# Attention biases in a two-layer hybrid decoder: made one head group at a time, spread in DRAM four heads at a time

## The chip, the cores and the metric

The kernel runs on one core of a Trainium2 chip. The time is device microseconds of one execution of the whole program; the kernel before has a median of 2954.24 us over three runs (2948.36 to 2954.89). The engines are TensorE (PE; its weight loads are listed as PEld), VectorE (DVE), ScalarE (ACT), GpSimd (POOL) and SyncE (SP). SP and POOL issue the DMAs.

## The reference

One sequence of 1024 tokens with 1024 channels passes two layers. Layer 0 mixes tokens by a gated delta rule, layer 1 by dilated sliding-window attention; each is followed by a SwiGLU, and each sub-layer has an RMS norm with shift, scale and gate from a condition. The change touches layer 1 alone:

```python
DSW_GROUPS = ((128, 1), (512, 4), (2048, 16))      # (window, dilation); 8 heads of 64 channels in each
proj = (h @ w_in).reshape(Bsz, S, 3, 3, 8, 64)     # queries, keys, values; group; head
q = rms_norm(proj[:, :, 0], q_gain) * 64 ** -0.5
k = rms_norm(proj[:, :, 1], k_gain)
v = proj[:, :, 2]
# in each group: query t attends to keys t, t-d, ..., t-window
logits = q @ k + bias_table[t5_causal_bucket(dist * dilation)]   # one bias for each head and distance
p = softmax(where(valid, logits, -inf)); o = p @ v
# the three groups' outputs are merged by their softmax denominators, then @ w_out
```

For each group and head the bias depends on the distance between query and key only. For a tile of 128 queries and 256 keys it is a band matrix: row p is a vector of 383 numbers shifted by p.

## The kernel before, in words

All products are float32 made of three products of a high and a low part (`split3`: `wh*hh + wh*hl + wl*hh`). The program is written in an order; a planner then orders each engine's instructions by its own account of when each is ready, earlier written ones first, and each engine runs its instructions strictly in that order. SP's queue of DMA issues is such an order too: an issue that waits holds up all issues behind it.

Layer 1 works in six units (`units`, line 1731): group 0, 2, 1, and in each the lower and the upper four heads (`hq`). A unit computes its queries, keys and values (`attn_proj`, line 1538, called at 1733 to 1735), each 1024 tokens by 256 channels in four pieces `t2` of 256 tokens, and then goes over eight tiles of 128 queries (`attn_unit`, line 1571): logits into a PSUM bank `pt`, logits plus bias with a row maximum on VectorE (line 1606), exponentials on ScalarE, transposes into bank `pp`, products with the values into bank `ob`. For the first unit, pieces 0 and 1 of all three kinds are computed in the stage ahead (`pre`), and lie in PSUM until they are copied out. Queries and keys are squared, summed and scaled (lines 1551 to 1556), transposed in bank `tq`, and copied to SBUF (lines 1566, 1568).

Weights are loaded by SP in pieces of 256 KB into raw tiles `wraw` (line 185); ScalarE makes the high part (line 187), VectorE and POOL in turn subtract it to make the low part (`lo_of`, line 161). Two kinds of buffers take turns, two weight units each (`wpools`): one with four raw tiles and one, `wps`, with a single raw tile, so that there a load starts only when the piece before it has been split. The first unit's values and the second unit's keys use `wps`.

PSUM has eight banks, in this stage `banks(pd="a", pt="b", pp="c", tq="d", ob="e")`, with two banks behind a, b and c and one behind d and e. Bank b holds the keys made ahead when the stage begins.

The biases come from `bias_rows` (line 1491), called behind the first unit's values (line 1737). For each group, one product of the table with a one-hot matrix (`oh`, loaded at line 1486) in a bank `pt` gives 8 vectors of 383; VectorE copies them to a tile `bv`, whose buffers it shares with the squares of the queries and keys (`sqv`, three buffers), and POOL stores them in DRAM (`v_d`). Then, for each group, one POOL transfer within DRAM copies each vector 128 times (`b_d`, 1532 KB). `attn_unit` loads a tile of four heads' biases from there, with each row shifted by one number (line 1577, on SP), into one of two buffers.

Of the kernel before, what the change touches and what calls it, by code (L numbers as in the profile page):

```python
# [10 lines left out]
F32 = mybir.dt.float32  # L11
# [6 lines left out]
P = 128  # L18
# [14 lines left out]
VL = 383  # L33
# [35 lines left out]
def trunk(tc, A, out, stop=None):  # L69
    nc = tc.nc  # L70
    V, G, ACT, SP = nc.vector, nc.gpsimd, nc.scalar, nc.sync
# [28 lines left out]
    def pool(name, bufs=1, **k):  # L100
        return tc.tile_pool(name=name, bufs=bufs, reuse_waits="tile", **k)
# [5 lines left out]
    def scratch(name, shape):  # L107
        if stop is not None:
            return nc.dram_tensor(name, shape, F32, kind="ExternalOutput").ap()
        return dr.tile(list(shape), F32, name=name)  # L110

    ps = es.enter_context(pool("ps", 1, space=PSUM))
    bank = {}
# [12 lines left out]
    def pt():  # L126
        return bank["pt"]()
# [10 lines left out]
    def rsqrt(o, i, n, half=0):  # L138
        G.tensor_tensor(o, i, pw[:, half, :n], ALU.pow)
# [393 lines left out]
    with ExitStack() as ga:  # L533
# [482 lines left out]
        src = [[], []]  # L1016
# [363 lines left out]
    def attn_products(g, hq, kind, t2s, hT, pd_, wk=None):  # L1380

        wk = wk or attn_weights(g, hq, kind)
        for t2 in t2s:
            o = pd_()
            for j in range(2):
                hf, tk = toks(g, 2 * t2 + j)
                split3(o[:, j * 256:(j + 1) * 256],
                       [((hT[hf][k][0][:, tk], hT[hf][k][1][:, tk]),
                         (wk[k // 4][0][:, k % 4], wk[k // 4][1][:, k % 4])) for k in range(KT)])
            yield (kind, t2), o  # L1390
# [65 lines left out]
    def quad(kind):  # L1456
        return qp.tile([P, 2048], F32, name="qkv", tag="qkv%d" % kind)
# [13 lines left out]
    with ExitStack() as da:  # L1471
# [3 lines left out]
        ap_ = da.enter_context(pool("da", 2))  # L1475
        ROW = DH + 2

        bias_d = [scratch("v_d", (3, 8, VL)), scratch("b_d", (3, 8, P, VL))]
        og_d = scratch("og_d", (S, 2, 2, 4 * ROW))
        ou0 = ap_.tile([P, NCH, 2, 4, ROW], F32, name="ou0", bufs=1)  # L1480

        def t2k(name, *shape, tag=None, bufs=2):
            return ap_.tile([P, *shape], F32, name=name, tag=tag or name, bufs=bufs)

        oh = ap_.tile([BUCKETS + 1, 3, VL], F32, name="oh", tag="gl")
        SP.dma_start(oh.rearrange("p g n -> p (g n)"), A["k_oh"])
        rel = ap_.tile([BUCKETS + 1, 24], F32, name="rel", bufs=1)
        V.memset(rel[BUCKETS:BUCKETS + 1], 1.0)
        SP.dma_start(rel[0:BUCKETS], A["rel_bias"])

        def bias_rows():

            for g in range(3):
                b = pt()
                PE.matmul(b[0:8, 0:VL], rel[:, g * 8:(g + 1) * 8], oh[:, g], start=True, stop=True)
                bv = ap_.tile([8, VL], F32, name="bv", tag="sqv", bufs=3)
                V.tensor_copy(bv, b[0:8, 0:VL])
                G.dma_start(bias_d[0][g], bv)
            for g in range(3):
                G.dma_start(bias_d[1][g], bias_d[0][g][:, None, :].to_broadcast([8, P, VL]))  # L1500

        def reorder(views):

            spare = [t_[:, j] for t_ in (ap_.tile([P, 2, HALF], F32R, name="hs", tag="gl") for _ in range(2))
                     for j in range(2)] if not spares else spares
            for k in range(KT):
                new = [[], []]
                for i in range(2):
                    old = [hT[h][k][i] for h in range(2)]
                    for at in range(2):  # L1510
                        new[at].append(spare.pop(0))
                        for h in range(2):
                            o, x = views(new[at][i], at, old[h].bitcast(F32), h)
                            if i == 0:
                                ACT.activation(o, x, AF.Copy)  # L1515
                            else:
                                V.tensor_copy(o, x)
                    spare += old
                for h in range(2):
                    hT[h][k] = tuple(new[h])  # L1520
            spares[:] = spare
# [16 lines left out]
        def attn_proj(g, hq, kind):  # L1538
            if (g, hq) == (0, 0):
                todo = chain((((kind, t2), pre[kind, t2]) for t2 in range(2)),  # L1540
                             attn_products(g, hq, kind, range(2, 4), hT, pd, pre["w"] if kind == 0 else None))
            else:
                todo = attn_products(g, hq, kind, range(4), hT, pd)
            res = quad(kind)
            for (_, t2), o in todo:
                if kind == 2:
                    ACT.activation(res[:, t2 * HALF:(t2 + 1) * HALF], o, AF.Copy)
                    continue
                sqv = t2k("sqv", 8, DH, bufs=3)
                ov = o.rearrange("p (a b) -> p a b", b=DH)  # L1550
                ACT.activation(sqv, ov, AF.Square)
                ss = ap_.tile([P, 2, 8], F32, name="ssa", tag="ssa", bufs=3)
                V.tensor_reduce(ss[:, 0], sqv, axis=mybir.AxisListType.X, op=ALU.add)
                V.tensor_scalar(ss[:, 0], ss[:, 0], 1.0 / DH, EPS, op0=ALU.mult, op1=ALU.add)
                rsqrt(ss[:, 1], ss[:, 0], 8)
                V.tensor_tensor(sqv, ov, ss[:, 1, :, None].to_broadcast([P, 8, DH]), ALU.mult)
                qf = sqv.rearrange("p a b -> p (a b)")
                b = bank["tq"]()
                for hp in range(2):
                    for j in range(2):  # L1560
                        PE.transpose(b[:, (hp * 2 + j) * P:(hp * 2 + j + 1) * P],
                                     qf[:, j * 256 + hp * P:j * 256 + (hp + 1) * P], ident)
                d = res.rearrange("p (h t c) -> p h t c", h=2, t=NCH)[:, :, 2 * t2:2 * t2 + 2]
                bv = b.rearrange("p (h t c) -> p h t c", h=2, t=2)
                if kind == 0:
                    ACT.activation(d, bv, AF.Copy)
                else:
                    ACT.activation(d, bv, AF.Copy, scale=gqk)
            return res

        def attn_unit(g, hq, q, k, v, half_done):
            bias = ap_.tile([P, 4, 256], F32, name="bias", tag="bias")
            src = bias_d[1][g, hq * 4]

            def load(p0, n, c0):

# [13 lines left out]
            for at, t in enumerate(order):  # L1590
# [23 lines left out]
                ob = bank["ob"]()  # L1614
                for i in range(2):
                    b = bank["pp"]()
                    bv = b.rearrange("p (h w c) -> p h w c", h=2, w=2)
# [9 lines left out]
                    for hp in range(2):  # L1627
                        h = 2 * hp + i
                        for w in range(w0, 2):
                            PE.matmul(ob[:, h * DH:(h + 1) * DH], pT[:, hp, w], vv[:, t - 1 + w, h * DH:(h + 1) * DH],  # L1630
                                      start=w == w0, stop=w == 1)
# [13 lines left out]
        src = [[], []]  # L1645
# [84 lines left out]

        units = [(g, hq) for g in (0, 2, 1) for hq in range(2)]
        for g, hq in units:
            q = attn_proj(g, hq, 0)
            k = attn_proj(g, hq, 1)
            v = attn_proj(g, hq, 2)
            if (g, hq) == units[0]:
                bias_rows()
            if (g, hq) in ((0, 1), (2, 1)):
                reorder(mod16 if g == 0 else mod4)
            attn_unit(g, hq, q, k, v, half_done if (g, hq) == units[-1] else None)  # L1740
# [57 lines left out]
def program(inputs, stop=None):  # L1798
    import concourse.bacc as bacc
    nc = bacc.Bacc("TRN2", target_bir_lowering=False, num_devices=1, dynamic_dma_scratch_size=8192)  # L1800
    arrays = {n: np.ascontiguousarray(inputs[n]) for n in _INS}
    arrays["k_sq"], arrays["k_oh"] = shape_constants()
    aps = {n: nc.dram_tensor(f"in_{n}", a.shape, mybir.dt.from_np(a.dtype), kind="ExternalInput").ap()
           for n, a in arrays.items()}
    out = nc.dram_tensor("out_0", (1, S, D), F32, kind="ExternalOutput").ap()
    with tile.TileContext(nc, schedule_with_timeline_sim=True) as tc:
        trunk(tc, aps, out, stop)
    return nc, {f"in_{n}": a for n, a in arrays.items()}
# [7 lines left out]
```

## Time and profile before

| | |
|---|---|
| median of three runs | 2954.24 us |
| the profiled execution | 2960.85 us |
| its span, first to last instruction | 2959.0 us |
| mean granted TensorE clock | 0.961 |
| PE busy | 2774.2 us, 94% |
| PEld busy | 2355.6 us, 80% |
| DVE busy | 1686.9 us, 57% |
| ACT busy | 1078.8 us, 36% |
| POOL busy | 584.4 us, 20% |
| weight loads of layer 1's attention | 68 of 256.0 KB, 2.9 us from issue to landing |

Times inside the span count from its start. A share of busy time is an average over stages with different limits; a stage is read from its own window. [...] A DMA issue is short; its transfer is told by the time to landing.

### The profile page before, as it was taken

Reading aid. Unit: us, or ns where it says so; the run is one execution under the profiler, and the core shown is the slowest. Engines: PE = TensorE matmul, PEld = TensorE weight load, DVE = VectorE, ACT = ScalarE, POOL = GpSimd, SP = SyncE. Lnnn points to the kernel's source line nnn. Section 1 sums busy time; section 2 is a strip of 40 time slices with the busy share of each in tenths; the row PEclk is TensorE's granted clock in tenths of the full one; section 3 lists DMA queues with packets and bytes.
Section 4 is the critical chain, followed back from the end, with each engine's and each line's share of the span. In section 5 each row is a group of like instructions: output and inputs, shape, how many; then the busy total and the mean of one; then the engine's idle time right before and its main releaser. Section 6 shows DMA issues by size and latency. Waiting matters only on the chain.

```text
span 2959.0 us, 40301 instructions
## 1 busy us (share of the span) xinstructions
PE 2774.2 (94%) x15207; PEld 2355.6 (80%) x15207; DVE 1686.9 (57%) x3387; ACT 1078.8 (36%) x2187; POOL 584.4 (20%) x644
## 2 busy tenths in 40 slices
PE   6989888888999999999999899999978999999999
PEld 5767776776877888878889789999966788888887
DVE  7875676664586666677454333332368655557443
ACT  5432333332363333332133453353335433334110
POOL 2151415141202111100014112322211111111000
PEclk8989999899999999999999989999979999999999
DMA  7333432234734344375222311111223222237211
GB/s 260 95 92 111 113 88 72 57 90 142 236 113 142 122 136 126 121 262 184 73 75 75 92 29 32 51 48 46 85 91 105 75 82 85 80 114 235 86 43 57
DMA packets 299679, 312.16 MB, mean 105 GB/s; under 512 B 35683, under 2 KB 219747, under 8 KB 299484
## 3 DMA queue, kind: packets, MB, share of 16 engines
q1 hardware_dynamic: 288140, 278.16, 30.7%
q0 software_dynamic: 11344, 31.43, 3.3%
q8 instruction: 119, 1.95, 0.3%
q14 instruction: 76, 0.62, 0.1%
HBM read 250.55 MB, written 63.66 MB: 106 GB/s over the span
## 4 chain that ended last, share of the span: by engine, by line
PE 68%; DMA 10%; DVE 9%; POOL 3%; ACT 3%; issue 3%; SPq 0%; DVEq 0%; POOLq 0%; ACTq 0%
PE pd L79 33%; PE u L79 14%; PE v L79 7%; PE pt L79 4%; PE y L79 4%; DMA araw<-in_w_ada 3%; PE ob L79 2%; POOL U L802 1%; POOL Ut L800 1%; PE p L79 1%; DVE w L161 1%; DVE acc L227 1%; DMA E<-gs_d 1%; PE sc L79 1%; PE pp L79 1%
## 5 line engine op out<-in xcount | busy, mean ns | idle before, releaser
L79 PE MATMUL pd<-hl,w 128*128 128x512 f32 x4248 | 1072.3, 405 | 22.0 <-ACT w L187 7.9
L79 PEld LDWEIGHTS pd<-hl,w 128*128 128x128 f32 x4248 | 799.5, 194 | 189.9 <-ACT w L187 8.8
L79 PE MATMUL pd<-w,hl 128*128 128x256 f32 x2880 | 390.6, 288 | 4.5 <-ACT hl L1515 3.8
L79 PEld LDWEIGHTS pd<-w,hl 128*128 128x128 f32 x2880 | 363.3, 194 | 11.7 <-ACT hl L1515 4.9
L79 PE MATMUL u<-hx,wo 128*128 128x512 f32 x1056 | 254.6, 391 | 5.1 <-ACT ft L1252 3.7
L161 DVE TENSOR_TENSOR w<-wraw,w 128x512 fp32r<-128x512 f32 (+1 forms) x243 | 197.0, 822 | 93.4 <-ACT w L187 65.6
L79 PEld LDWEIGHTS u<-hx,wo 128*128 128x128 f32 x1056 | 198.5, 188 | 47.5 <-ACT ft L1252 4.1
L187 ACT ACTIVATE w<-wraw 128x512 fp32r<-128x512 f32 (+1 forms) x171 | 107.8, 645 | 214.4 <-DMA wraw<-in_gdn_w_in 100.8
L227 DVE SCALAR_TENSOR_TENSOR acc<-araw,vecT,acc 128x512 f32<-128x512 f32 x140 | 110.0, 786 | 92.1 <-DMA araw<-in_w_ada 91.5
L1362 DVE SCALAR_TENSOR_TENSOR qkv<-pd,modT,qkv 128x512 f32<-128x512 f32 x96 | 71.5, 749 | 123.0 <-PE pd L79 123.0
L161 DVE TENSOR_TENSOR wo<-ss,wo 128x512 fp32r<-128x512 f32 x88 | 83.6, 957 | 92.4 <-ACT wo L1199 90.7
L79 PE MATMUL u<-hl,w 128*128 128x512 f32 x528 | 130.3, 396 | 0.7 <-DVE qkv L487 0.7
L79 PE MATMUL v<-hl,wo 128*128 128x512 f32 x528 | 126.9, 390 | 0.4 <-DVE ft L1254 0.4
L79 PE MATMUL y<-hl,w 128*128 128x512 f32 x528 | 127.2, 390 | 0.0
L79 PE MATMUL v<-hx,wo 128*128 128x512 f32 x528 | 126.6, 389 | 0.0
L79 PE MATMUL u<-hl,wo 128*128 128x512 f32 x480 | 117.5, 394 | 5.0 <-ACT ft L1252 5.0
L1606 DVE CUSTOM_DVE_ANT_0 p<-pt,bias 128x128 f32<-128x128 f32 (+1 forms) x192 | 57.4, 348 | 112.8 <-PE pt L79 65.9
L688 DVE SCALAR_TENSOR_TENSOR yv<-raw,vecT,yv 128x512 f32<-128x512 f32 x144 | 114.2, 793 | 12.8 <-ACT yv L686 12.0
L79 PEld LDWEIGHTS u<-hl,w 128*128 128x128 f32 x528 | 100.9, 192 | 22.3 <-issue 1.1
L1222 POOL TENSOR_TENSOR ss<-wraw 128x512 f32<-128x512 f32 x30 | 42.5, 1416 | 385.1 <-PE u L79 310.0
L161 POOL TENSOR_TENSOR w<-wraw,w 128x512 fp32r<-128x512 f32 (+1 forms) x35 | 50.4, 1441 | 345.0 <-ACT w L187 345.0
L79 PEld LDWEIGHTS v<-hl,wo 128*128 128x128 f32 x528 | 99.0, 188 | 21.4 <-DVE ft L1254 0.8
(377 smaller groups left out, 4267.6 us busy)
## 6 DMA issues: line engine op xcount, KB each, us to landing
araw<-in_w_ada SPq DMA_DIRECT2D x160, 256.0 KB, 2.8
wraw<-in_w_ffn_in SPq DMA_DIRECT2D x66, 512.0 KB, 3.9
wraw<-in_dsw_w_in SPq DMA_DIRECT2D x68, 256.0 KB, 2.9
wraw<-in_w_ffn_out SPq DMA_DIRECT2D x34, 512.0 KB, 4.8
wraw<-in_gdn_w_in SPq DMA_DIRECT2D x66, 256.0 KB, 2.9
ft<-a_d SPq DMA_DIRECT2D x44, 256.0 KB, 3.8
qkv<-in_w_ffn_in SPq DMA_DIRECT2D x22, 512.0 KB, 3.9
qkv<-a_d SPq DMA_DIRECT2D x44, 256.0 KB, 3.4
```

Of the source, the lines that this page charges most:

```text
L79: i = f(*a, **k)
L161: e.tensor_tensor(o, x, hi.bitcast(F32), ALU.subtract)
L187: ACT.activation(hi, raw, AF.Copy)
L227: V.scalar_tensor_tensor(acc, raw, condT[:, k:k + 1], acc, op0=ALU.mult, op1=ALU.add)
L688: V.scalar_tensor_tensor(yv, raw[:, i:i + HALF], convT[:, i, ct:ct + 1], yv, op0=ALU.mult, op1=ALU.add)
L800: G.tensor_tensor(t, U[:, 0:m, m:m + 1].to_broadcast([64, m, n]), U[:, m:m + 1, m + 1:32].to_broadcast([64, m, n]), ALU.mult)
L802: G.tensor_tensor(U[:, 0:m, m + 1:32], U[:, 0:m, m + 1:32], t, ALU.add)
L1222: (V if i < 2 else G).tensor_tensor(s["s1"], a21, a22, ALU.add)
L1362: V.scalar_tensor_tensor(xt, o, modT[:, l, 5, n:n + 1], xt, op0=ALU.mult, op1=ALU.add)
L1606: V.tensor_tensor_reduce(p_[i][:, hp, c0:], lg[i][:, hp * 256 + c0:hp * 256 + 256], bias[:, h, c0:], 1.0, -3.0e38, ALU.add, ALU.max, orow[ ...
```

## The change

`bias_rows` makes one group at a time. It is called three times within the first unit: group 0 behind the queries, group 2 behind the keys, group 1 behind the values. Its product goes to a bank `ob`. Each group has DRAM tensors of its own, and the upper and lower four heads each have their own spread tensor and their own transfer (766 KB). Store and spreads are issued by SP in place of POOL. `attn_unit` loads from the spread of its own four heads.

```diff
-        bias_d = [scratch("v_d", (3, 8, VL)), scratch("b_d", (3, 8, P, VL))]
+        bias_d = [scratch("v%d_d" % g, (8, VL)) for g in range(3)]
+        spread_d = [[scratch("b%d%d_d" % (g, q), (4, P, VL)) for q in range(2)] for g in range(3)]
@@
-        def bias_rows():
-
-            for g in range(3):
-                b = pt()
-                PE.matmul(b[0:8, 0:VL], rel[:, g * 8:(g + 1) * 8], oh[:, g], start=True, stop=True)
-                bv = ap_.tile([8, VL], F32, name="bv", tag="sqv", bufs=3)
-                V.tensor_copy(bv, b[0:8, 0:VL])
-                G.dma_start(bias_d[0][g], bv)
-            for g in range(3):
-                G.dma_start(bias_d[1][g], bias_d[0][g][:, None, :].to_broadcast([8, P, VL]))
+        def bias_rows(g):
+
+            b = bank["ob"]()
+            PE.matmul(b[0:8, 0:VL], rel[:, g * 8:(g + 1) * 8], oh[:, g], start=True, stop=True)
+            bv = ap_.tile([8, VL], F32, name="bv", tag="sqv", bufs=3)
+            V.tensor_copy(bv, b[0:8, 0:VL])
+            SP.dma_start(bias_d[g], bv)
+            for q in range(2):
+                SP.dma_start(spread_d[g][q], bias_d[g][q * 4:q * 4 + 4, None, :].to_broadcast([4, P, VL]))
@@
-            src = bias_d[1][g, hq * 4]
+            src = spread_d[g][hq][0]
@@
-            q = attn_proj(g, hq, 0)
-            k = attn_proj(g, hq, 1)
-            v = attn_proj(g, hq, 2)
-            if (g, hq) == units[0]:
-                bias_rows()
+            qkv = []
+            for kind in range(3):
+                qkv.append(attn_proj(g, hq, kind))
+                if (g, hq) == units[0]:
+                    bias_rows((0, 2, 1)[kind])
+            q, k, v = qkv
```

## Rows read from the trace of the kernel before

**Rows 1.** The page: busy time of TensorE; the chain that ended last, by engine.
```profile
PE 2774.2 (94%) x15207; PEld 2355.6 (80%) x15207; DVE 1686.9 (57%) x3387; ACT 1078.8 (36%) x2187; POOL 584.4 (20%) x644
...
PE 68%; DMA 10%; DVE 9%; POOL 3%; ACT 3%; issue 3%; SPq 0%; DVEq 0%; POOLq 0%; ACTq 0%
```
**Rows 2.** Waits, 1560 to 1720: engine, line, releaser: total us, times, longest.
```profile
DVE p L1606 <- DMA bias<-b_d: 16.9, 1, 16.9
...
POOL b_d L1500 <- DMA v_d<-bv: 13.8, 1, 13.8
...
PE pt L79 <- DVE ou L1606: 9.8, 1, 9.8
```
**Rows 3.** Waits of SP's queue of issues, the same stretch.
```profile
SPq L1577 <- DMA b_d<-v_d: 23.3, 1, 23.3
```
**Rows 4.** Chain of waits, 1560 to 1720: start us, us, what.
```profile
1613.29 2.65 DMA v_d<-bv
1615.94 1.79 issue
1617.73 18.39 DMA b_d<-v_d
1636.18 4.76 DMA bias<-b_d
1641.88 2.28 PE pt L79 x8
```
**Rows 5.** Windows: length, busy PE, PEld, DVE, ACT, POOL (instructions); clock, DMA share, GB/s.
```profile
1632.20:1641.80 9.60, 0.00 (x0) 0.00 (x0) 0.70 (x7) 0.00 (x0) 1.08 (x1) 0.74 0.85 214
1641.90:1647.00 5.10, 5.10 (x21) 4.45 (x22) 3.59 (x15) 2.55 (x10) 1.66 (x1) 0.50 0.67 165
```
**Rows 6.** Chain of waits, 1590 to 1612: loads of the first values' weights.
```profile
1595.19 2.78 DMA wraw<-in_dsw_w_in
...
1604.24 2.75 DMA wraw<-in_dsw_w_in
1606.99 0.02 issue
```
**Rows 7.** Timeline, 1585 to 1670: start us, us, engine, line, operation [idle before, releaser].
```profile
1588.10 6.47 PE L79 MATMUL pd<-w,hl 128*128 128x256 f32 x52
...
1607.30 1.45 PE L79 MATMUL pt<-oh,rel 33*8 33x383 f32 x4
...
1609.10 3.47 PE L79 MATMUL pd<-w,hl 128*128 128x256 f32 x27
...
1611.77 0.54 DVE L1497 COPY bv<-pt 8x383 f32<-8x383 f32 x1
...
1641.10 0.29 DVE L1606 CUSTOM_DVE_ANT_0 p<-pt,bias 128x128 f32<-128x128 f32 x1 [16.90 <-DMA bias<-b_d]
```
**Rows 8.** DMA, 1620 to 1636: queue: packets, MB, share of 16 engines; issues to landing.
```profile
q0 software_dynamic: 1283, 3.01, 93.9%
...
v_d<-bv POOLq DMA_DIRECT2D x1, 12.0 KB, 14.5
```
**Rows 9.** DMA, 1643 to 1653, with only the third spread in flight.
```profile
q0 software_dynamic: 296, 1.33, 47.2%
...
wraw<-in_dsw_w_in SPq DMA_DIRECT2D x1, 256.0 KB, 8.7
```
**Rows 10.** DMA, 1638 to 1639.2: the third spread's issue.
```profile
b_d<-v_d POOLq DMA_DIRECT2D x1, 1532.0 KB, 15.6
```
**Rows 11.** Windows of the projections' products alone: length, busy PE (instructions), clock, DMA.
```profile
1609.00:1622.30 13.30, 12.22 (x96) 1.00 0.48 132
1622.30:1692.90 70.60, 29.21 (x191) 0.93 0.39 95
```
**Rows 12.** Timeline of SP's issues, 1660 to 1690.
```profile
1660.22 0.37 SPq L185 DMA_DIRECT2D wraw<-in_dsw_w_in  x1
1679.86 1.30 SPq L1577 DMA_DIRECT2D bias<-b_d  x2
```

## The prediction

> **What bounds the kernel now.** I read the page first. TensorE is busy for 94% of the span and carries 68% of the chain of waits [rows 1], so only two things move the time: stretches in which TensorE stands still, and stretches in which it runs at the lower of its two clock levels. Then the waits in the stretch that holds the edit, 1560 to 1720 us: TensorE has one long entry, 9.8 us, a logits matmul waiting for VectorE to empty the bank [rows 2]. Then the chain through that stretch, to see what VectorE itself waited for: the first bias vector lands, POOL issues the spread, it takes 18.39 us to land, the bias load takes another 4.76, and TensorE goes on at 1641.88 [rows 4]. VectorE meanwhile waited 16.9 us for that load [rows 2], and SP, which issues it, stood 23.3 us behind the spread [rows 3]. Last the stretch cut in windows, to price the stall. Between 1632.2 and 1641.8 TensorE does nothing. [...] **The bias path costs 9.8 + 2.5 = 12.3 us now, and nothing in the change can gain more there.**
>
> **Part by part.**
>
> *The spread leaves the path to the first logits.* It is issued after the queries of the first unit, not after its values. The queries' products end at about 1594.5 (row 1588.10) and VectorE comes to the first logits at 1641.1 - 16.9 = 1624.2 [rows 7]; the old chain from vector to loaded bias is 2.65 + 1.79 + 18.39 + 4.76 = 27.6 us [rows 4]. From 1597 that ends at 1624.6 even if no step of it is faster. I take the 9.8 us as gained; less is gained only if the load is late for another reason, below.
>
> *Where the first bias now starts.* The former bank `pt` was held by products made ahead, `ob` is free from the start of the stage. TensorE has work without a gap to 1594.5 [rows 7]; the bias matmul ranks behind the queries, so I put it there. Two matmuls, at most half of the 1.45 us that four took, then a VectorE copy of 0.54 us [rows 7] and some queueing: SP issues the vector at about 1597 and waits 2.65 us for it to land [rows 4]. The two spreads go out at about 1601; bounds 1590 (a gap in the planner's account before the queries end) and 1604. Matmuls and copies are as many as before and only move. TensorE does them ahead of 1609, where it waits for weights anyway, so I cost them at nothing; without that cover it is 1.5 us.
>
> *POOL gives up six issues and SP takes nine.* POOL's 13.8 us wait for the third vector [rows 2] held up no chain piece [rows 4], so nothing is gained. An SP issue takes 0.37 us (row 1660.22) [rows 12]; nine are 3.3 us on a queue that mostly waits, nothing by itself. What costs is what stands behind them: SP issues every weight load, and its transfers share one queue.
>
> *What stands behind the first pair.* The first unit's values have their weights split from a single raw buffer: load, ScalarE copy, a subtraction, next load. Three loads leave 4.2 to 4.9 us apart, the last at 1604.24; each takes 2.75 to 2.78 us; the last lands at 1606.99 [rows 6], and the values' first matmul starts at 1609.10, right behind the bias matmuls and four transposes [rows 7]. This chain has no slack: whatever delays its last load stalls TensorE by as much. The pair at 1601 lies ahead of that load. If the pair goes earlier, it lies ahead of two or three of the loads, which then follow it one after the other, so the sum hardly changes.
>
> *How long the pair holds the load.* The trace shows that a transfer with eight outermost rows does not use all engines: with two spreads in flight POOL's queue took 93.9% of 16 engines [rows 8], with the third alone 47.2% [rows 9], so eight engines each. The third took 15.6 us from issue to landing [rows 10], and a 256 KB weight load issued beside it took 8.7 us [rows 9]. That a queue is served in order shows in the third 12 KB vector: 14.5 us [rows 8], because it lay behind two spreads in POOL's queue, against 2.65 for the first. A transfer of four rows has half the bytes on, I take it, half the engines, so each half takes as long as the third whole one, 15.6 us. Side by side, the pair lands at 1601 + 15.6 = 1616.6; one behind the other, with 2.6 us of fixed cost counted once, at 1601 + 15.6 + 13.0 = 1629.6. The load of 1604.24 lands some 0.5 us later: 1617 to 1630 in place of 1607, a stall of 10 to 23 us. The trace does not say on which four engines the second half runs, and with fewer engines at DRAM one may be faster than 13 us per half. I take the middle, 16 us.
>
> [...]
>
> *The clock.* The new stall is longer than the old one, so I charge TensorE the same 2.5 us of half-rate work behind it that [rows 5] show; the clock term cancels. If the new stall is too short to bring the clock down, 2.5 us more are gained.
>
> *Behind the first unit.* The second group's vector waits in SP's queue behind the first pair, SP stands still for it, and the pairs of groups 2 and 1 follow: at 16 to 28 us each they last until about 1665 to 1690. The loads of that time are those of the second unit's keys and values. Its queries have their weights already, and the keys start only when 288 products after 1609 are done, at 1693 (96 and 191 of them, one record missing) [rows 11], while the keys' last load leaves at 1660.22 now [rows 12]: some 30 us of cover. Group 2's bias load is issued at 1679.86 [rows 12]. I cost these at nothing; the bound is 5 us.
>
> *Sum.* 16.0 (values late) - 9.8 (old stall) - 2.5 + 2.5 (clock) = +6.2 us on the profiled execution's 2960.85, so 2967.0. That execution lies 6.6 us above the median of the runs, 2954.24; on the median the forecast is 2960.4.
>
> **The rivals.**
>
> 1. *Faster: the weight loads are not held.* It decides at one point: whether the values' last load leaves ahead of the pair, or TensorE has the next unit's queries to do meanwhile. For it: 3 us separate 1601 from 1604.24, and the planner's own account of ready times may differ from the trace by as much. Against: everything of the bias ranks ahead of the values. Price: 9.8 to 12.3 us gained, about 2943.
>
> 2. *Spread over all 16 engines.* For it: SP is another issuer, and 16 engines moved 3.01 MB in 16 us [rows 8]. Then the pair's 1.57 MB take 8.3 + 2.6 us, the load lands at 1612, the stall is 5: 5 - 9.8 = -4.8, 2949.5. Against: the 47.2% of [rows 9].
>
> 3. *Both halves on the same four engines,* one behind the other at full price: a stall of 23, 23 - 9.8 = +13, 2967.5. For it: the order within a queue [rows 8]. Against: two spreads in a row took different halves of the engines in POOL's queue. [...]
>
> 4. *The second group's pair also passes the last load.* It needs the bias matmul of group 2 before about 1599, inside the keys' products, where no gap of TensorE shows: another 13 to 26 us on top, about +26, 2980.
>
> **How the numbers follow.** The case of the forecast (held by the first pair, stall 10 to 20, 0 to +10 us) 0.36; rival 1 0.25; rival 2 0.13; rival 3 0.18; rival 4 0.08. A measurement of this kernel tells 0.2%, 5.9 us, from no change. Faster: nearly all of rival 1 and a third of rival 2, 0.27. Slower: half of the forecast's case and rivals 3 and 4, 0.44. The rest, 0.29, is within. The likeliest case alone gives 2954 to 2964. The range leaves out the end of rival 1 and most of rival 4: 2942.5 to 2974.
>
> **What would show it.** Right: no stall at the first logits, and a new one of 10 to 23 us ahead of the first unit's values, ended by a weight load that took over 10 us; spreads of 766 KB on SP with a DMA share of about 0.25 or 0.5 while they run; the clock at 0.50 for some us after that stall. Wrong, each in its place: no stall near 1609 (rival 1), a DMA share near 0.9 during one pair (rival 2), halves landing 13 us apart (rival 3), two pairs ahead of the values (rival 4). The forecast is wrong altogether if TensorE still stops at the first logits, or if the time moves in a stretch far from 1580 to 1700 us.

## The result

The changed kernel takes 2990.66 us (median of four runs, 2982.46 to 2993.98) against 2954.56 us of the kernel before: ratio 1.0127, 95% interval 1.0108 to 1.0146. It is slower by 36 us where 6 us were forecast, and outside the range. The executions profiled differ by 33.1 us (2993.98 against 2960.85).

TensorE's waits in the changed kernel, 1560 to 1800 us (columns as in [rows 2]):

```profile
PE pt L79 <- DVE ou L1606: 24.3, 1, 24.3
PE tq L79 <- ACT qkv L1568: 10.3, 1, 10.3
...
PE ob L79 <- DMA rel<-in_rel_bias: 1.2, 1, 1.2
```

One stall of 9.8 us [rows 2] has become two, of 10.3 and 24.3 us. The chain of waits through that stretch says what they are made of (columns as in [rows 4]):

```profile
1601.43 17.83 DMA wraw<-in_dsw_w_in
...
1633.75 16.85 DMA v_d<-bv
1650.62 0.60 SPq L1500
1651.27 1.68 SPq L1500
1653.00 18.89 DMA wraw<-in_dsw_w_in
1671.91 0.64 ACT w L187
1672.57 0.69 DVE w L161
...
1674.00 2.07 PE pt L79 x4
...
1755.58 14.65 PE pd L79 x122
```

A weight load of 256 KB takes 17.83 us from issue to landing, where 2.78 were usual [rows 6]; a store of 12 KB takes 16.85 us, where 2.65 were usual [rows 4]; a second weight load takes 18.89. The last line is the same run of 122 products that the kernel before has here:

```profile
1725.93 14.64 PE pd L79 x122
```

By there 29.65 us are lost. Up to the end of layer 1's attention products the distance stays between 29.6 and 30.3 us. The other 3 us of this one pair of executions come later, far from the edit, and are less than executions of one kernel differ.

The order of SP's issues (start, length, operation):

```profile
1597.23 0.39 SPq L185 DMA_DIRECT2D wraw<-in_dsw_w_in  x1
1597.72 3.20 SPq L1500 DMA_DIRECT2D b_d<-v_d  x2
1601.43 8.23 SPq L185 DMA_DIRECT2D wraw<-in_dsw_w_in  x1
1610.01 9.11 SPq L1577 DMA_DIRECT2D bias<-b_d  x2
...
1628.93 3.98 SPq L1500 DMA_DIRECT2D b_d<-v_d  x2
1633.75 8.50 SPq L1498 DMA_DIRECT2D v_d<-bv  x1
1650.62 2.33 SPq L1500 DMA_DIRECT2D b_d<-v_d  x2
1653.00 30.20 SPq L185 DMA_DIRECT2D wraw<-in_dsw_w_in  x4
```

Each slow transfer stands behind a pair of spreads: the values' load at 1601.43 (the third of their four pieces) behind group 0's, the third vector at 1633.75 behind group 2's, the second unit's key weights at 1653.00 (the second of four pieces) behind group 1's. And between 1633.75 and 1650.62 SP issues nothing more: the issue of that vector lasts 8.50 us, and then SP waits for it to land.

How many engines the pairs run on is read from the DMA share while nothing else is in flight (1640 to 1650 us, two transfers of four rows issued; columns as in [rows 8]):

```profile
q1 hardware_dynamic: 561, 0.84, 24.9%
```

A quarter of 16: four engines for two transfers, so the halves run one behind the other. That they use the same four is the simplest reading of it; the trace does not number the engines. 0.84 MB in 10 us, the last of them nearly idle, makes about 9 us for a half of 0.784 MB.

Windows of the changed kernel (columns as in [rows 5]):

```profile
1610.40:1620.50 10.10, 0.00 (x0) 0.00 (x0) 0.00 (x0) 1.21 (x3) 0.50 (x1) 0.74 0.51 147
1620.60:1626.50 5.90, 5.07 (x25) 4.45 (x26) 3.47 (x6) 3.32 (x7) 4.17 (x4) 0.50 0.58 177
1626.60:1649.60 23.00, 23.00 (x165) 20.08 (x164) 7.32 (x32) 9.83 (x26) 3.41 (x3) 0.95 0.34 112
1649.70:1674.00 24.30, 0.00 (x0) 0.00 (x0) 1.40 (x6) 0.63 (x1) 0.00 (x0) 0.57 0.24 76
1674.10:1678.50 4.40, 4.40 (x15) 3.56 (x16) 1.68 (x10) 4.17 (x15) 1.31 (x1) 0.50 0.25 61
1678.60:1723.00 44.40, 44.40 (x358) 41.18 (x357) 16.77 (x54) 19.14 (x58) 6.13 (x4) 0.98 0.07 18
```

In the fourth window nearly every engine stands while the DMA share is 0.24, four engines' worth. The clock: at a granted clock of 0.50 a product `pd` of 256 columns takes TensorE 0.26 us (8.3 us for 32 of them, 1759.6 to 1779 in the kernel before), at 1.00 0.13 us (13.0 us for 101, 1594 to 1609), so half of the time at 0.50 counts as lost. 5.07 us of work at half rate behind the first stall and 4.40 behind the second cost 2.5 + 2.2 us, and the clocks of 0.95 and 0.98 another 1.2 + 0.9: 6.8 us, where the old stall cost 2.5. Sum of the stretch: 10.3 + 24.3 for the new stalls, 1.2 + 0.8 for small waits that the kernel before does not have, - 9.8 for the old stall, + 4.3 for the clock = 31.1 us, against 29.65 measured.

### The profile page after: what moved, and what is told of

It reads as the page before. It is cut to its first block, busy times and chain, and to the rows that moved or that the text cites. A ratio compares the mean times of both kernels' runs of the same rounds, so it can differ in the third digit from the quotient of the medians.

```text
span 2992.2 us, 40296 instructions
## 1 busy us (share of the span) xinstructions
PE 2781.0 (93%) x15207; PEld 2364.9 (79%) x15207; DVE 1685.5 (56%) x3387; ACT 1079.9 (36%) x2187; POOL 578.2 (19%) x638
## 4 chain that ended last, share of the span: by engine, by line
PE 60%; DVE 6%; DMA 5%; ACT 2%; issue 1%; SPq 0%; POOL 0%; DVEq 0%; ACTq 0%; POOLq 0%
PE pd L79 29%; PE u L79 14%; PE v L79 7%; PE y L79 4%; PE pt L79 2%; PE ob L79 2%; DMA wraw<-in_dsw_w_in 1%; PE pp L79 1%; PE tq L79 1%; DMA gl<-og_d 1%; DMA v_d<-bv 1%; DVE w L161 1%; DMA araw<-in_w_ada 1%; DVE wo L161 1%; DVE hl L161 1%
## 5 line engine op out<-in xcount | busy, mean ns | idle before, releaser
L688 DVE SCALAR_TENSOR_TENSOR yv<-raw,vecT,yv 128x512 f32<-128x512 f32 x144 | 113.2, 786 | 11.5 <-ACT yv L686 10.5
L139 POOL TENSOR_TENSOR ssa<-ssa,pw 128x8 f32<-128x8 f32 x48 | 80.4, 1676 | 185.1 <-DVE ssa L1554 180.3
```

What stands on the lines that cost most here:

```text
L688: V.scalar_tensor_tensor(yv, raw[:, i:i + HALF], convT[:, i, ct:ct + 1], yv, op0=ALU.mult, op1=ALU.add)
```

## The experiments

Ratios are to the kernel before, of runs on the same chip (its median there was 2947 to 2949 us). The theory formed from the two traces, A: a spread of four rows runs on four DMA engines on SP's queue, always the same four, and everything issued behind it on that queue waits for it. Rival B: SP's queue as such. Rival C: the planner's new order on the compute engines. The planner orders anew for each kernel, and its order moves with most edits. Only three pairs below have one and the same order on every engine: the changed kernel and its copies outermost, POOL's two shapes, and the two shapes at the old place.

**The shape alone, in the changed kernel.** The 128 copies become the outermost dimension. The instruction order of all engines is the changed kernel's, SP's too but for the shape of six transfers.

```diff
-                SP.dma_start(spread_d[g][q], bias_d[g][q * 4:q * 4 + 4, None, :].to_broadcast([4, P, VL]))
+                SP.dma_start(spread_d[g][q].rearrange("h p n -> p h n"), bias_d[g][None, q * 4:q * 4 + 4, :].to_broadcast([P, 4, VL]))
```

> The changed kernel with one edit: each spread's dimensions are turned, so that the 128 copies are outermost in place of the four heads. Every engine's order of instructions stays as in the changed kernel; only the six SP transfers have another shape. Theory A (four rows run on four engines, and the weight loads lie behind them in SP's queue): a pair takes about 8 + 2.6 us in place of 20, the values' load behind it lands near 1610 in place of 1619, the third vector waits under 9 us in place of 16.9, the stalls of 10.3 and 24.3 us shrink to under 4 and under 8; the time is 2945 to 2962 us, 1% below the changed kernel. Rival B (it is SP's queue as such: it stands still for each vector and the loads wait behind, whatever the engines): above 2980. Rival C (the planner's new order on TensorE, ScalarE and VectorE costs it): above 2980 too, since that order is the same here.

Measured: 2944.42 us, ratio 0.9994 (0.9980 to 1.0008), the same as before the change. All 36 us are gone with the shape alone. Its DMA share with one pair in flight (1595 to 1601 us), and what is left in its chain of waits:

```profile
q1 hardware_dynamic: 1005, 1.44, 89.5%
```
```profile
1626.41 6.93 DMA wraw<-in_dsw_w_in
1633.37 0.64 ACT w L187
```

The same load of the second unit's keys that took 18.89 us takes 6.93, and the longest wait of TensorE that the kernel before does not have is 2.0 us. The shape is the cause; the four engines of A fit it. B and C fall as causes by themselves: queue and order are the same in both kernels.

**The queue, in the changed kernel: POOL issues.** The planner's order differs a little from the changed kernel's on TensorE, VectorE and ScalarE.

```diff
-            SP.dma_start(bias_d[g], bv)
+            G.dma_start(bias_d[g], bv)
...
-                SP.dma_start(spread_d[g][q], bias_d[g][q * 4:q * 4 + 4, None, :].to_broadcast([4, P, VL]))
+                G.dma_start(spread_d[g][q], bias_d[g][q * 4:q * 4 + 4, None, :].to_broadcast([4, P, VL]))
```

> The changed kernel with the stores and the four-row spreads issued by POOL in place of SP. Theory A: the weight loads are not in POOL's queue any more; they share at most some engines with a spread and take up to 9 us beside it, as one did before. 2943 to 2960 us, no stall of 24 us. Rival C (the order on TensorE, ScalarE and VectorE): above 2975, though the planner's order is not quite the same here. A stall at the first logits would say that POOL's own waits for the vectors delay the biases again.

Measured: 2958.04 us, ratio 1.0032 (1.0018 to 1.0045). Inside the expectation, at its upper end. A pair on POOL's queue took 47.9% of 16 engines (1605 to 1612 us): eight, so there the halves run side by side on four each. Still TensorE stands 10.0 us in the first tiles:

```profile
PE pp L79 <- ACT p L1612: 10.0, 1, 10.0
PE pt L79 <- DVE ou L1606: 5.4, 1, 5.4
```

Two delays add up there, both ahead of a key load that ScalarE has to split among the tiles. The load takes 9.2 us beside the third pair. And it leaves late, at 1642.85, because POOL's subtraction of the piece before, which frees the single raw tile, stands behind POOL's own bias work: ScalarE was done with that piece at 1635.5, but POOL waits 13.8 us for the third vector, issues the third pair and subtracts at 1641.54.

**Both: POOL issues, copies outermost.** The order of all engines is that of the kernel just shown.

```diff
-                G.dma_start(spread_d[g][q], bias_d[g][q * 4:q * 4 + 4, None, :].to_broadcast([4, P, VL]))
+                G.dma_start(spread_d[g][q].rearrange("h p n -> p h n"), bias_d[g][None, q * 4:q * 4 + 4, :].to_broadcast([P, 4, VL]))
```

> As the kernel with POOL's four-row spreads, and each spread turned so that the 128 copies are outermost; every engine's order is the same as there, only six POOL transfers have another shape. Theory A: nothing of the bias is late and no load is held for long; the old stall of 9.8 us and its 2.5 us of half clock are gone: 2940 to 2950 us, faster than before by 0.2 to 0.4%. If the shape doesn't matter on POOL's queue, as long as loads have their own queue, it is the same as the four-row one within 3 us.

Measured: 2946.96 us, ratio 0.9993 (0.9976 to 1.0010). The expected gain of 0.2 to 0.4% does not show. The shape does matter on POOL's queue, against the second half of the expectation: 0.4% between these two. The wait of the first tiles is 5.1 us here; it stands behind a key load of 7.4 us beside the third pair, which again leaves behind POOL's wait for the third vector (8.25 us to land).

**One early group in place of three, SP and shape as changed.**

```diff
-                if (g, hq) == units[0]:
+                if (g, hq, kind) in ((0, 0, 0), (0, 1, 1), (0, 1, 2)):
                     bias_rows((0, 2, 1)[kind])
```

> The changed kernel, but only group 0's biases are made in the first unit; those of groups 2 and 1 come behind the second unit's keys and values. Theory A: the stall of 10.3 us ahead of the first values stays (its pair stands where it stood), the stall of 24.3 us in the first tiles goes, since no second and third pair lie ahead of the second unit's key weights; a later pair costs 0 to 10 us where it meets a load that is split just in time: 2958 to 2975 us. If each pair costs what it did wherever it stands: about 2985 to 2990.

Measured: 2972.81 us, ratio 1.0093 (1.0071 to 1.0115), in the expected range. TensorE's waits, 1560 to 1800 us:

```profile
PE pd L79 <- ACT qkv L1547: 16.4, 3, 11.0
PE tq L79 <- ACT qkv L1568: 11.2, 1, 11.2
```

The stall ahead of the first values stays (11.2 us), the one of 24.3 goes, and a new one of 11.0 us comes with the later pairs, behind a weight load of 17.78 us. That the cost follows the pairs to another place is what A says; it is more than the 10 us that were allowed for a later pair.

**Only the third group later.** The list of places reads `((0, 0, 0), (0, 0, 1), (0, 1, 2))` in the same line.

> The changed kernel with one group moved: group 1's biases come behind the second unit's values, groups 0 and 2 stay where the change put them. Theory A (the 24.3 us stall is the third vector waiting behind the second pair, then the second unit's key weights behind the third pair, with ScalarE and VectorE standing at their split): the stall of 10.3 us stays, the stall of 24.3 us shrinks to under 9, since the key weights then lie behind the second pair alone; the third pair costs 0 to 11 us where it now meets weight loads. 2962 to 2982 us (before taken as 2948). Rival D (the second pair alone makes the stall): the stall stays above 18 us and the time above 2983.

Measured: 2971.75 us, ratio 1.0082 (1.0053 to 1.0111).

```profile
PE tq L79 <- ACT qkv L1568: 10.5, 1, 10.5
PE pd L79 <- ACT qkv L1547: 9.8, 2, 8.9
PE pt L79 <- DVE ou L1606: 6.8, 3, 5.7
```

10.5 us stay, 24.3 shrink to 5.7, and 8.9 come up where the third pair now stands. Rival D falls: the second pair alone makes 5.7 us, and the rest of the 24.3 needs the third vector's wait and the third pair.

**One transfer of eight heads for each group, on SP.** `spread_d` gets one tensor of eight heads for each group, and `attn_unit` reads from it at `hq * 4` (these lines are left out here). The planner's order differs a little from the changed kernel's on TensorE, VectorE, ScalarE and SP.

```diff
-            for q in range(2):
-                SP.dma_start(spread_d[g][q], bias_d[g][q * 4:q * 4 + 4, None, :].to_broadcast([4, P, VL]))
+            SP.dma_start(spread_d[g], bias_d[g][:, None, :].to_broadcast([8, P, VL]))
```

> The changed kernel with one transfer of eight heads for each group in place of two of four, still on SP. Theory A (engines by the number of outermost rows): the transfer runs on eight engines, about 11 + 2.6 us for a group in place of 20; the values' load is late by 3 to 5 us in place of 12, the second stall is 8 to 14 us in place of 24.3: 2955 to 2972 us. If the two transfers of a pair had run side by side, one transfer of eight rows would be no faster than the pair: 2982 to 2990.

Measured: 2954.23 us, ratio 1.0017 (1.0000 to 1.0033), slightly better than expected. Its chain of waits, 1580 to 1690 us, and the DMA share with one spread alone (1624 to 1630 us):

```profile
1599.11 9.53 DMA wraw<-in_dsw_w_in
...
1621.42 9.40 DMA v_d<-bv
...
1631.60 11.69 DMA wraw<-in_dsw_w_in
```
```profile
q1 hardware_dynamic: 792, 1.05, 51.3%
```

The same three transfers stand on the chain, at 9.53, 9.40 and 11.69 us in place of 17.83, 16.85 and 18.89: eight engines in place of four. "Each four heads by a transfer of their own" goes with nearly twice these times: the ratio goes from 1.0127 to 1.0017, 32 of the 36 us. The small changes of order go with it in this pair; that the order is not what counts is shown by the shape alone, above.

**The move alone.** Places and bank as in the change; POOL issues, for each group, a store and one spread of eight heads (`spread_d` and `attn_unit` as in the experiment before, left out here).

```diff
-            SP.dma_start(bias_d[g], bv)
+            G.dma_start(bias_d[g], bv)
...
-            for q in range(2):
-                SP.dma_start(spread_d[g][q], bias_d[g][q * 4:q * 4 + 4, None, :].to_broadcast([4, P, VL]))
+            G.dma_start(spread_d[g], bias_d[g][:, None, :].to_broadcast([8, P, VL]))
```

> The move alone: one group at a time at the change's three places and its bank, but POOL issues a store and one spread of eight heads for each group, as before the change. Theory A: no weight load lies behind a spread in a queue; a load beside one takes up to 9 us on the eight shared engines, so some stalls of 3 to 10 us may stand, as with POOL's four-row spreads: 2944 to 2960 us, ratio 0.998 to 1.004. Rival C (the new order on the engines costs the time): above 2975.

Measured: 2951.61 us, ratio 1.0016 (1.0003 to 1.0030). The earlier place takes away the old stall and gives back one of 11.8 us in the first tiles. It is made as with POOL's four-row spreads: POOL waits 12.1 us for the third vector behind the second spread, only then subtracts the piece that ScalarE had split 9 us before, and the key load that this lets go takes 8.45 us beside the third spread. This kernel and the one with one transfer of eight heads on SP differ by the issuing queue and what the planner made of that, and take the same time (1.0016 and 1.0017); with the copies outermost the two queues do so too (0.9993 and 0.9994). At the change's places the queue matters for the four-row pairs alone.

**The queue, at the old place.** The planner's order changes a little here too.

```diff
-                G.dma_start(bias_d[0][g], bv)
+                SP.dma_start(bias_d[0][g], bv)
...
-                G.dma_start(bias_d[1][g], bias_d[0][g][:, None, :].to_broadcast([8, P, VL]))
+                SP.dma_start(bias_d[1][g], bias_d[0][g][:, None, :].to_broadcast([8, P, VL]))
```

> The kernel before with its stores and spreads of eight heads issued by SP in place of POOL; place and shape as before. Theory A (what is behind a spread in SP's queue pays): the first spread alone lands after 13 us and the first logits wait less than 9.8 us, but the second unit's key weights lie behind the second or third spread and ScalarE and VectorE stand at their split in the first tiles, 5 to 15 us: ratio 1.000 to 1.005. If SP's queue is harmless at the old place: 0.997 to 0.999.

Measured: 2956.30 us, ratio 1.0033 (1.0015 to 1.0050), in the expected range; the chain now holds key loads of 10.44 and 12.35 us, as A has it. The loss itself came by another way than the 5 to 15 us of standing that were expected: TensorE stands for 3.6, 3.6 and 1.6 us there, in sum 1 us less than the 9.8 of the kernel before, but it works at half rate for 17.1 us of the stretch that holds the edit, where the kernel before did for 5.1. That makes 6 us.

**The shape alone, at the old place.**

```diff
-                G.dma_start(bias_d[1][g], bias_d[0][g][:, None, :].to_broadcast([8, P, VL]))
+                G.dma_start(bias_d[1][g].rearrange("h p n -> p h n"), bias_d[0][g][None].to_broadcast([P, 8, VL]))
```

> The kernel before with its three spreads of eight heads turned so that the 128 copies are outermost; place and queue (POOL) as before. Theory A: the first spread has all 16 engines to itself ahead of the second, lands after 8.3 + 2.6 = 11 us in place of 18.4, and the first logits wait 2 to 6 us in place of 9.8: 4 to 9 us gained, ratio 0.997 to 0.9985. Rival (bytes at DRAM set the time, not engines): the first two spreads still land after 18 us, ratio 0.999 to 1.001.

Measured: 2942.40 us, ratio 0.9981 (0.9968 to 0.9994). The chain, where [rows 4] had 18.39 and 4.76:

```profile
1613.57 11.58 DMA b_d<-v_d
1625.22 7.20 DMA bias<-b_d
```

The first spread takes 6.8 us less; 2.4 of these go back to the bias load, which now runs beside the second spread; the stall is 5.3 us in place of 9.8.

**All in one.** POOL issues, copies outermost, group 0 behind the first unit's queries, groups 2 and 1 behind the second unit's keys and values. The lines that move the issues to POOL and turn the shape are as shown above and left out here.

```diff
                 qkv.append(attn_proj(g, hq, kind))
-                if (g, hq) == units[0]:
-                    bias_rows((0, 2, 1)[kind])
+                if (g, hq) == units[0] and kind == 0:
+                    bias_rows(0)
+                if (g, hq) == units[1] and kind:
+                    bias_rows((0, 2, 1)[kind])
```

> POOL issues the stores and the spreads, each spread is turned so that the 128 copies are outermost, only group 0 is made in the first unit, and groups 2 and 1 come behind the second unit's keys and values. Theory A: group 0 is ready before the first logits, and no other spread is in flight while the second unit's key weights are loaded, so that the 5.1 us stall that the kernel with three early spreads on POOL still had goes too: 2934 to 2944 us with before at 2948, 0.2 to 0.4% faster. If a stall that the spreads make comes back with the later groups: 2944 to 2952, the same as before.

Measured: 2941.73 us, ratio 0.9979 (0.9967 to 0.9992): 0.2% faster than the kernel before, as much as the shape alone at the old place. No wait of TensorE in the stretch that the biases make is above 2 us.

**The stretch by itself.** One execution of each kernel was traced, so the part that holds the edit can be compared without the rest of the program. From the last product `p` of the stage ahead to the first product of the second unit's keys it takes (1581.92 to 1693.02 us in the kernel before; the two kernels that move narrow pairs behind the stretch are left out):

| kernel | us |
|---|---|
| before | 111.1 |
| changed | 140.8 |
| changed, copies outermost, SP | 106.2 |
| four rows, POOL | 119.9 |
| copies outermost, POOL | 106.7 |
| eight heads, SP | 117.4 |
| the move alone (eight heads, POOL) | 114.8 |
| old place, SP | 118.2 |
| old place, copies outermost | 106.1 |
| all in one | 101.6 |

So in this stretch the copies outermost gain some 5 us over the kernel before at either place, and all in one 9.5 of the 12.3 us that the old bias path cost; the medians show 1 to 7 us of it. Behind the stretch the traces differ by something else: TensorE is at half rate for 20.5 us in the kernel before (from 1759.6), in the changed kernel and in its version with the copies outermost, and not at all at that place in four others, among them the two fastest. No run ties that to the biases, and single executions can differ by it.

## Why the prediction was wrong

- *The old stall goes: right.* VectorE starts the first tile at 1626.44 without waiting for a bias load.
- *Where the first pair is issued: about right.* Forecast 1601, measured 1597.72. The planner put the bias matmul at 1583.29, ahead of the queries, where it waited 1.2 us for the table to land; I had it behind them and free. The cover that I gave it was misread: the kernel before has no wait for weights ahead of 1609, TensorE is busy for 15.00 of 15.00 us from 1594 to 1609. Nothing hangs on it, since the products only move. The VectorE copy came at 1594.80, so the pair was no earlier for it. It does stand ahead of the values' last two weight loads: the third leaves at 1601.43 and is held, the last at 1621.30, once the third has been split.
- *How long the pair holds the load: the mechanism right, the size near its lower bound.* Bounds 10 to 23 us, taken 16, measured 10.3. The halves do run one behind the other on four engines, which I gave 0.18 as rival 3: SP's two transfers together took 24.9% of 16, POOL's pair 47.9%. That a transfer of four rows takes half the engines of one of eight was my estimate, and these shares fit it. But a half took about 9 us on its four engines, where I had carried over 13 from a transfer on eight. The way to TensorE was not the forecast one either: it stops at transposes into bank `tq`, not at the values' first product (1623.64), because ScalarE's copy out of that bank stands behind the split of the late load:

```profile
1619.29 0.63 ACT L187 ACTIVATE w<-wraw 128x512 fp32r<-128x512 f32 x1 [14.04 <-DMA wraw<-in_dsw_w_in]
1619.83 0.67 ACT L1568 ACTIVATE qkv<-tq,gqk 128x512 f32<-128x512 f32 x1
```

- *Behind the first unit: wrong, and this is the step that failed.* "I cost these at nothing; the bound is 5 us." I had the pairs lasting to 1665 or later, and SP standing for the second vector. I then asked when TensorE needs the second unit's key weights, found 30 us of cover, and stopped. The question was where the split of these weights stands in ScalarE's and VectorE's orders. It stands among the first unit's tiles, in the middle of the third tile's logits. The kernel before shows it already: ScalarE splits these weights at 1643.84, 1653.96 and 1658.84, and the first tile starts at 1641.10 [rows 7]. (The load of 1660.22 that I took for the keys' last is the next unit's first; theirs leaves at 1655.96. The cover is 4 us longer by that, and nothing else changes.) These are ScalarE's and VectorE's rows of the changed kernel at that point:

```profile
1671.91 0.63 ACT L187 ACTIVATE w<-wraw 128x512 fp32r<-128x512 f32 x1 [28.08 <-DMA wraw<-in_dsw_w_in]
```
```profile
1672.57 0.69 DVE L161 TENSOR_TENSOR w<-wraw,w 128x512 fp32r<-128x512 f32 x1 [27.06 <-ACT w L187]
1673.18 0.42 DVE L1606 CUSTOM_DVE_ANT_0 p<-pt,bias 128x256 f32<-128x256 f32 x1
```

  ScalarE waits 28.08 us for the load, VectorE waits for ScalarE, the logits wait behind VectorE's split, and TensorE waits for the logits' bank: 24.3 us for weights whose first product is nearly 50 us away (1722.6). Three delays add up in front of that load: SP waits 16.85 us for the third vector behind the second pair, the third pair is issued first, and the load waits 18.89 us behind it. That later groups follow so closely is the same mistake: I priced each pair at its own place and not as a queue in which the next vector waits for the pair before.
- *The clock: forecast to cancel.* With two stalls it cost 4.3 us more than before. The 2.5 us of the old stall are half of the 5.10 us that TensorE worked at a granted clock of 0.50 behind it [rows 5].
- *Rivals 1, 2 and 4* did not happen. With the failed step put right and the first stall at its measured size, the sum is the 31.1 us above.

## What to carry to other kernels

Try a broadcast's copies as the outermost dimension of its transfer: with the 128 copies outermost in place of the four heads a pair on SP's queue took 89.5% of 16 engines in place of 24.9%, and two kernels with the same instruction order on every engine differed by 1.3% through that alone. Keep a slow transfer out of the queue that carries just-in-time loads: behind a pair of four rows two loads of 256 KB took 17.83 and 18.89 us here, where 2.78 was usual. A store whose landing the queue waits for costs whatever lies ahead of it there too, 16.85 us here in place of 2.65. Look in the same way at an engine that issues transfers and also computes just in time: POOL's wait of 13.8 us for a vector held its own part of the split. To price a late load, look for the first in-order instruction that touches it on any engine, not for the matmul that needs it.

## What the hardware showed that was not expected

- SP's issues themselves became long: 8.23, 8.50 and 10.33 us (the last at 1653.00) for one issue behind a pair, where 0.37 is usual [rows 12]. With one transfer of eight heads the longest is 3.13 us, and with the copies outermost they are 0.3 to 0.7 us again. That a backlog of the transfers ahead does it is a guess; no run tried it by itself.
- Three short stalls (3.6, 3.6 and 1.6 us) went with 17.1 us of work at a granted clock of 0.50, one of 9.8 us with 5.1.
- Two spreads of four rows took four engines together on SP's queue (24.9% of 16) and eight on POOL's (47.9%).
- On SP's queue DRAM rows of 1532 bytes moved at nearly the same rate for each engine that was busy, on four engines (0.84 MB in 10 us at 24.9% of 16) and on eight (1.05 MB in 6 us at 51.3%): 0.021 MB in each us of a busy engine.
